# A macaron hybrid layer on one core: outputs of the down projection added in DRAM by DMAs, and a third Strassen set in two more pairs of groups of each FFN

## The chip, the cores and the metric

The kernel runs on one core of a Trainium2 chip. The metric is the time of one execution on the device in microseconds (us). Five engines run in parallel, each its own instructions in order: TensorE (PE: matmuls into PSUM; PEld is its weight load), VectorE (DVE), ScalarE (ACT), GpSimd (POOL) and SyncE (SP, here only issuing DMAs). They wait for each other through semaphores. DMAs issued by GpSimd can add to what stands at their destination in DRAM; those are called accumulating below.

## What is computed

One decoder layer on 256 tokens of width 2048, in float32: a half-step SwiGLU FFN (inner width 5632), a layer norm, a mixer (sliding-window attention beside a convolution, one projection in and one out), a layer norm, a second half-step FFN, a layer norm.

```python
def swiglu_ffn(x, w_gate, w_up, w_down):
    h = jax.nn.silu(x @ w_gate) * (x @ w_up)
    return h @ w_down
...
    x = layer_norm(DEEPNORM_ALPHA * x + 0.5 * swiglu_ffn(x, ffn1_w_gate[l], ffn1_w_up[l], ffn1_w_down[l]),
                   ln1_g[l], ln1_b[l])
...
    x = layer_norm(DEEPNORM_ALPHA * x + mixed, ln2_g[l], ln2_b[l])
    x = layer_norm(DEEPNORM_ALPHA * x + 0.5 * swiglu_ffn(x, ffn2_w_gate[l], ffn2_w_up[l], ffn2_w_down[l]),
                   ln3_g[l], ln3_b[l])
```

## The kernel before

**Precision.** Each float32 operand is split into a high and a low part. ScalarE casts the high part (line 170), VectorE subtracts it for the low part (line 174), and each product of two blocks is three matmuls into the same PSUM bank (`mm3`, lines 677 to 679).

**The FFN's stages.** The inner width is worked in three parts (`PARTS`). Each part has an up stage and then a down stage. The up stage computes gate and up columns in groups of 512 columns (256 of each); groups are numbered 0 to 21, and after the first two (FFN 1) or four (FFN 2) plain groups they come in pairs: 2, 4 and 6 in part one (4 and 6 in FFN 2), 8, 10, 12, 14 in part two, 16, 18, 20 in part three. `pair` makes one. The down stage multiplies the part's inner columns by the down weights. Its output has 4 column blocks of 512 (`NC_`), taken two at a time: column pair `c` = 0, then `c` = 2. In parts one and two both column pairs go through `down_by_sums`; in part three only the first does.

**Sets.** A pair of groups, and a column pair of a down stage, is 8 sets (6 in part three's down stage) of two blocks along the contraction for two token blocks and two column blocks. A "C" set is made plainly with 8 products, 24 matmuls. An "S" set is made after Strassen and Winograd with 7 products, 21 matmuls. An S set's weights need four more subtractions on VectorE (line 188, tiles `sum` and `more`), and three wide and two narrow splits become its four sources: one of 1024 columns as loaded, one of two times 512, one of 1024 and one of 512. A C set needs two splits of 1024. `UP` holds three orders of a pair of groups: the first two have two S sets, the third has three. `up_of` picks one: the first for the pair after the plain groups, the third for the first pair of parts two and three (groups 8 and 16), the second otherwise. `KINDS` gives the down stage's order, "SCCSCSCC" in parts one and two.

**Banks.** `by_sums` holds eight banks of PSUM. Products 1, 5, 6 and 7 occur in S sets alone; after the last S set, `shared` makes four partial sums of them (tiles `part`): ScalarE copies bank 1 scaled by `factor` (line 944), VectorE adds banks 6, 5, 7 and 5 (line 938; line 1077 in the up stage). Banks 2, 4, 3 and 0 go on collecting in the two C sets behind. `out` is called for banks 2 and 4 while the last set runs and for banks 3 and 0 at its end; in the down stage that is `leave`, where VectorE adds the bank to its partial sum (line 938) and GpSimd writes the tile to DRAM: plainly in FFN 1's part one (line 964), accumulating in the other three (line 962). The destination `side` is `y0` or `y1`. The next column pair or pair of groups begins at once in the same banks: its first products are 1, 5, 6, 7, then 2, 4, 3.

**Buffers and order.** The partial sums come from the buffers tagged "z", of which there are `ZB` = 5, as do the activations of the up stage and the sums of the hidden columns. `Steps` plans VectorE's and ScalarE's order: `pace`, called per product, takes the product's time from an estimate of VectorE's backlog, and while that is short lets further weights be split, up to `LEAD` = 7 sources ahead of their use. Weights arrive by SP in four raw buffers (`RAW_BUFS`) or, for S sets, in the tile `more`. In FFN 1, `keep_tokens` reads the layer's input in eight pieces and adds each to `y0` by an accumulating DMA of GpSimd (line 458), at fixed steps; the last falls in part two's first column pair of the down stage. After the last shared sums of an FFN, `tokens_back` loads the sums back from DRAM. GpSimd also writes and reads the transposed hidden columns (lines 1044, 1046).

Of the kernel before, what the change touches and what calls it, by code (L numbers as in the profile page):

```python
# [9 lines left out]
F32 = mybir.dt.float32  # L10
# [4 lines left out]
ALU = mybir.AluOpType  # L15
# [3 lines left out]
P = 128  # L19
# [12 lines left out]
)  # L32
SUMMED = (0, 1, 2)
JG = 2
NC_ = D // 512
# [28 lines left out]
ZB = 5  # L64
# [9 lines left out]


def up_of(g, j0, plain):
    return 0 if g == plain else 2 if g == j0 // JG else 1


def blocks_of(columns):  # L80
    return lambda kind: BLOCKS["L" if kind == "S" and columns < NC_ else kind]
# [265 lines left out]
def hybrid_layer(  # L347
# [3 lines left out]
    nc = tc.nc  # L351
# [4 lines left out]
    act = ctx.enter_context(tc.tile_pool(name="act", bufs=1))  # L356
# [20 lines left out]
    def add_ffn(wu, wd, plain):  # L377
        for (j0, j1), kinds in zip(PARTS, KINDS):
            for g in range(j0 // JG, j1 // JG, 2):
                if g < plain:  # L380
                    sources.extend(wu[g + i, q, h] for i in range(2) for q in range(4) for h in range(2))
                else:
                    for t, kind in UP[up_of(g, j0, plain)]:
                        add_set(kind, [wu[g + i, t // 2, t % 2] for i in range(2)])
            for c in range(0, NC_, 2):
                if c > 0 and j1 == JT:
                    sources.extend(wd[c + i, t // 2, t % 2] for i in range(2) for t in range(j0 // 2, j1 // 2))
                    continue
                for t, kind in enumerate(kinds, j0 // 2):
                    add_set(kind, [wd[c + i, t // 2, t % 2] for i in range(2)])  # L390
# [531 lines left out]
    def down_by_sums(hh, hl, kinds, factor, side, more, columns, last):  # L922

        firsts = [sum(map(blocks_of(columns), kinds[:t])) for t in range(len(kinds))]
        places = {
            "S": ("21", "11", "22", "12", "S1", "S2", "S3", "S4")[-blocks_of(columns)("S"):],
            "C": ("21", "11", "22", "12"),
        }

        def blocks(t, name):  # L930
            n = firsts[t] + places[kinds[t]].index(name)
            return hh[:, n], hl[:, n]

        for c in range(0, columns, 2):
            tmp, places_ = [], {(0, 0): 0, (0, 1): 2, (1, 0): 1, (1, 1): 3}

            def add(out, ps, other):
                nc.vector.scalar_tensor_tensor(out=out, in0=ps, scalar=factor, in1=other, op0=ALU.mult, op1=ALU.add)  # L938
                st.vector(0.62, 0.3)

            def shared(bank, tmp=tmp):

                tmp.extend(act.tile([P, 512], F32, tag="z", name="part", bufs=ZB) for k in range(4))
                nc.scalar.mul(tmp[0], bank[1], factor)
                add(tmp[1], bank[6], tmp[0])
                add(tmp[2], bank[5], tmp[1])
                add(tmp[1], bank[7], tmp[1])
                add(tmp[3], bank[5], tmp[1])
                if last is not None:
                    last()  # L950

            def leave(at, ps, c=c, tmp=tmp):

                t = tmp[places_[at]]
                add(t, ps, t)
                if columns < NC_:
                    y = xts[0][:, 1 - at[0], (c + at[1]) * 512 : (c + at[1] + 1) * 512]
                    joins[1 - at[0], at[1]] = lambda: nc.vector.tensor_tensor(out=y, in0=y, in1=t, op=ALU.add)
                    return
                place = side[1 - at[0], :, (c + at[1]) * 512 : (c + at[1] + 1) * 512]  # L960
                if more:
                    nc.gpsimd.dma_start(place, t, accum_op=ALU.add)
                else:
                    nc.gpsimd.dma_start(place, t)

            by_sums(kinds, blocks, leave, shared)

    def ffn(xc, tag, skew, begun, prepare, finish, places, kept=None):
        with tc.tile_pool(name=f"ffn{tag}", bufs=2) as pool:
            st.act, st.make_places = act, places  # L970
            lhs = (xc[:, :, 0, :], xc[:, :, 1, :])
            xs = pool.tile([P, len(SUMMED), 2, 4, P], F32R, tag="xs", name="xs", bufs=1)

            def sums_of(n):

                k = 2 * SUMMED[n]
                full = act.tile([P, 2, 2, P], F32, tag="z", name="full", bufs=ZB)
                part = act.tile([P, 4, P], F32, tag="z", name="sums", bufs=ZB)
                both = [x_[:, k : k + 2].bitcast(F32) for x_ in lhs]
                nc.vector.tensor_tensor(  # L980
                    out=full.rearrange("p k b n -> p k (b n)"), in0=both[0], in1=both[1], op=ALU.add
                )
                block_sums(part, [full[:, 0, 0], full[:, 0, 1], full[:, 1, 0], full[:, 1, 1]])
                nc.scalar.copy(xs[:, n, 0], part)

                def lower():
                    nc.vector.tensor_tensor(out=xs[:, n, 1], in0=part, in1=xs[:, n, 0].bitcast(F32), op=ALU.subtract)
                    st.vector(0.6)

                if st.paced:  # L990
                    st.soon.append(lower)
                else:
                    lower()
# [10 lines left out]
            def up_blocks(t, name):  # L1004

                if name[0] == "S":
                    return [xs[:, SUMMED.index(t), i, int(name[1]) - 1] for i in range(2)]
                k, b = 2 * t + int(name[1]) - 1, 2 - int(name[0])
                return [x_[:, k, b * P : (b + 1) * P] for x_ in lhs]

            for part, ((j0, j1), kinds) in enumerate(zip(PARTS, KINDS)):
# [109 lines left out]
                while g < j1 // JG:  # L1121
                    if part == 1 and g == j0 // JG:
                        for m in range(2, len(SUMMED)):
                            st.at(4, lambda m=m: st.soon.append(lambda: sums_of(m)))
                    pair(g, UP[up_of(g, j0, plain)])
                    g += 2
                side = sides[xc is not xcat]
                down_by_sums(
                    hh, hl, kinds, 0.5, side, part > 0 or xc is not xcat, columns, (lambda: tokens_back(side)) if ends else None
                )  # L1130
# [466 lines left out]
```

## Time and profile before

| | |
|---|---|
| three runs, median (lowest to highest) | 1674.53 us (1673.40 to 1674.97) |
| the profiled execution | 1675.41 us, span 1673.6 us |
| granted TensorE clock | 0.998 |
| HBM | 349.64 MB read, 27.26 MB written, 225 GB/s |
| GpSimd's DMA queue (q0) | 16112 packets, 45.10 MB, 11.1% of 16 engines |
| ScalarE waits for VectorE's weight subtractions (line 188) | 177.8 us + 158.7 us in all |
| GpSimd waits for VectorE's outputs (line 938, write at line 962) | 172.2 us in all |

The span runs from the first to the last instruction. In the views below, a row of the timeline gives the start, the duration, the engine, the line and operation, the tiles written and read, and in brackets the idle time of the engine before it and who ended it. A row of the groups gives busy time, mean duration in ns, and idle time. A row of the windows gives busy time of each engine and its instructions in a stretch. Starts of matmuls are exact to some ten ns; their ends are modelled.

| stage (us from the span's start) | FFN 1 | FFN 2 |
|---|---|---|
| up, part one, pairs | 49 to 176 | 1052 to 1137 |
| down, part one | 176 to 259 | 1137 to 1220 |
| up, part two (pairs 8, 10, 12, 14) | 259 to 427 | 1220 to 1388 |
| down, part two | 427 to 512 | 1388 to 1471 |
| up, part three (pairs 16, 18, 20) | 512 to 638 | 1471 to 1597 |
| down, part three, first column pair | 638 to 669 | 1597 to 1628 |

### The profile page before, as it was taken

How to read it: one execution, taken by the hardware profiler on the slowest of the kernel's cores; microseconds unless marked ns; L12 is line 12 of the kernel's file. 1: busy time of each engine (PE TensorE's matmuls, PEld its weight loads, DVE VectorE, ACT ScalarE, POOL GpSimd, SP SyncE). 2: the span in 40 equal slices, each digit the busy share in tenths (PEclk: the TensorE clock that was granted, in tenths of full speed). 3: DMA queues.
4: the chain of work that ended last, by engine and by line, in shares of the span. 5: the costliest groups of instructions: out<-in, count | busy, mean ns of one | idle time of the engine just before them, and what ended most of it. 6: DMA issues, size and time to landing. Idle time of an engine off the chain costs nothing. (4 is left out here: it accounts for less than half of the span.)

```text
span 1673.6 us, 21985 instructions
## 1 busy us (share of the span) xinstructions
PE 1657.9 (99%) x7647; PEld 1375.4 (82%) x7647; DVE 1444.1 (86%) x2151; ACT 944.6 (56%) x1316; POOL 323.0 (19%) x302
## 2 busy tenths in 40 slices
PE   9999999999999999999999999999999999999997
PEld 7888888888878888888888888888888888888885
DVE  7899899888999987958888768799999888999877
ACT  6555555555555554676665466455555555556552
POOL 0100000111100001178996201000000000000012
PEclk9999999999999999999999999999999999999999
DMA  8667677677788666656654568666776666776665
GB/s 296 242 227 239 208 250 244 201 249 243 245 242 261 207 225 243 211 189 189 201 176 159 192 226 286 233 223 226 240 244 222 223 222 208 257 235 216 219 238 158
DMA packets 110976, 377.32 MB, mean 225 GB/s; under 512 B 13968, under 2 KB 14096, under 8 KB 110736
## 3 DMA queue, kind: packets, MB, share of 16 engines
q1 hardware_dynamic: 94032, 329.50, 56.6%
q0 software_dynamic: 16112, 45.10, 11.1%
q10 hardware_dynamic: 720, 1.31, 0.2%
q8 instruction: 60, 0.98, 0.2%
q14 instruction: 52, 0.43, 0.1%
HBM read 349.64 MB, written 27.26 MB: 225 GB/s over the span
## 5 line engine op out<-in xcount | busy, mean ns | idle before, releaser
L174 DVE TENSOR_TENSOR lo<-raw,hi 128x1024 fp32r<-128x1024 f32 x320 | 376.1, 1219 | 60.1 <-ACT hi L170 59.9
L677 PE MATMUL sum<-hi,xcat 128*128 128x512 f32 x1006 | 391.6, 389 | 0.4 <-DVE part L1077 0.4
L678 PE MATMUL sum<-lo,xcat 128*128 128x512 f32 x1006 | 391.4, 389 | 0.0
L679 PE MATMUL sum<-hi,xcat 128*128 128x512 f32 x1006 | 391.4, 389 | 0.0
L170 ACT CAST hi<-raw 128x1024 fp32r<-128x1024 f32 x320 | 321.5, 1047 | 59.2 <-DMA raw<-in_wd 19.0
L170 ACT CAST hi<-more 128x1024 fp32r<-128x1024 f32 (+1 forms) x210 | 190.6, 907 | 178.8 <-DVE more L188 158.7
L174 DVE TENSOR_TENSOR lo<-more,hi 128x1024 fp32r<-128x1024 f32 (+1 forms) x210 | 213.7, 1040 | 20.3 <-ACT hi L170 20.2
L677 PE MATMUL sum<-hi,hh 128*128 128x512 f32 x580 | 226.2, 390 | 1.3 <-DVE part L938 1.0
L678 PE MATMUL sum<-lo,hh 128*128 128x512 f32 x580 | 225.7, 389 | 0.0
L679 PE MATMUL sum<-hi,hl 128*128 128x512 f32 x580 | 225.7, 389 | 0.0
L677 PEld LDWEIGHTS sum<-hi,xcat 128*128 128x128 f32 x1006 | 188.8, 188 | 40.4 <-DVE part L1077 1.2
L679 PEld LDWEIGHTS sum<-hi,xcat 128*128 128x128 f32 x1006 | 188.8, 188 | 39.4
L678 PEld LDWEIGHTS sum<-lo,xcat 128*128 128x128 f32 x1006 | 188.8, 188 | 39.0
L253 ACT CAST hi<-raw 128x1024 fp32r<-128x1024 f32 (+1 forms) x156 | 158.5, 1029 | 93.2 <-PE acc L679 42.2
L256 POOL TENSOR_TENSOR lo<-raw,hi 128x1024 fp32r<-128x1024 f32 x73 | 175.9, 2436 | 111.6 <-ACT hi L253 104.8
L170 ACT CAST hi<-sum 128x512 fp32r<-128x512 f32 x140 | 86.8, 622 | 191.4 <-DVE sum L188 177.8
L1044 POOL DMA_DIRECT2D far<-hr x88 | 49.2, 564 | 753.0 <-DVE hr L1039 753.0
L677 PEld LDWEIGHTS sum<-hi,hh 128*128 128x128 f32 x580 | 108.8, 188 | 25.8 <-ACT hi L170 1.3
L679 PEld LDWEIGHTS sum<-hi,hl 128*128 128x128 f32 x580 | 108.9, 188 | 22.7
L678 PEld LDWEIGHTS sum<-lo,hh 128*128 128x128 f32 x580 | 108.9, 188 | 22.6 <-DVE lo L174 0.2
L1077 DVE TENSOR_TENSOR part<-sum,part 128x512 f32<-128x512 f32 x152 | 101.0, 687 | 26.8 <-PE sum L679 19.4
L256 DVE TENSOR_TENSOR lo<-raw,hi 128x1024 fp32r<-128x1024 f32 (+1 forms) x83 | 97.7, 1198 | 25.7 <-ACT hi L253 25.5
(210 smaller groups left out, 2436.1 us busy)
## 6 DMA issues: line engine op xcount, KB each, us to landing
raw<-in_wu SPq DMA_DIRECT2D x264, 512.0 KB, 5.0
raw<-in_wd SPq DMA_DIRECT2D x120, 512.0 KB, 5.3
more<-in_wu SPq DMA_DIRECT2D x84, 512.0 KB, 7.0
more<-in_wd SPq DMA_DIRECT2D x56, 512.0 KB, 7.3
raw<-in_win SPq DMA_DIRECT2D x52, 512.0 KB, 3.9
raw<-in_wout SPq DMA_DIRECT2D x32, 512.0 KB, 4.0
far<-hr POOLq DMA_DIRECT2D x88, 128.0 KB, 2.7
hf<-far POOLq DMA_DIRECT2D x22, 512.0 KB, 3.6
```

The lines of the kernel that those rows point to most:

```text
L170: self.nc.scalar.copy(hi, x_)
L174: self.nc.vector.tensor_tensor(out=lo, in0=x_, in1=hi.bitcast(F32), op=ALU.subtract)
L253: nc.scalar.copy(hi, raw)
L256: eng.tensor_tensor(out=lo, in0=raw, in1=hi.bitcast(F32), op=ALU.subtract)
L677: nc.tensor.matmul(ps, s_hi, m_hi, start=start, stop=False)
L678: nc.tensor.matmul(ps, s_hi, m_lo, start=False, stop=False)
L679: nc.tensor.matmul(ps, s_lo, m_hi, start=False, stop=stop)
L1044: nc.gpsimd.dma_start(far[:, :, t].rearrange("f r n -> r f n"), hr[32 * t : 32 * t + 32])
L1077: nc.vector.tensor_tensor(out=out, in0=ps, in1=other, op=ALU.add)
```

## The change

Two things. A tuple `THREE` names the pairs of groups with three S sets, so groups 12 and 20 of each FFN take the order of groups 8 and 16. And in the down stages of parts one and two, the four partial sums are written to DRAM as soon as `shared` has made them (as plain writes in FFN 1's part one, else accumulating); each output is then copied from its bank by ScalarE, times `factor`, into a "z" tile of its own (`rest`) and added in DRAM by an accumulating DMA. VectorE's last addition (line 938) falls away there. Part three's down stage stays as it was.

```diff
+THREE = (8, 12, 16, 20)
...
 def up_of(g, j0, plain):
-    return 0 if g == plain else 2 if g == j0 // JG else 1
+    return 0 if g == plain else 2 if g in THREE else 1
...
                 if last is not None:
                     last()
+                else:
+                    for at, k in places_.items():
+                        write(at, tmp[k], more)
+
+            def write(at, t, adds, c=c):
+
+                place = side[1 - at[0], :, (c + at[1]) * 512 : (c + at[1] + 1) * 512]
+                if adds:
+                    nc.gpsimd.dma_start(place, t, accum_op=ALU.add)
+                else:
+                    nc.gpsimd.dma_start(place, t)
 
             def leave(at, ps, c=c, tmp=tmp):
 
                 t = tmp[places_[at]]
-                add(t, ps, t)
                 if columns < NC_:
+                    add(t, ps, t)
                     y = xts[0][:, 1 - at[0], (c + at[1]) * 512 : (c + at[1] + 1) * 512]
                     joins[1 - at[0], at[1]] = lambda: nc.vector.tensor_tensor(out=y, in0=y, in1=t, op=ALU.add)
                     return
-                place = side[1 - at[0], :, (c + at[1]) * 512 : (c + at[1] + 1) * 512]
-                if more:
-                    nc.gpsimd.dma_start(place, t, accum_op=ALU.add)
-                else:
-                    nc.gpsimd.dma_start(place, t)
+                t = act.tile([P, 512], F32, tag="z", name="rest", bufs=ZB)
+                nc.scalar.mul(t, ps, factor)
+                write(at, t, True)
```

Since the third S set has two sources more than a C set, the sources behind it are numbered two higher, and lines below the first addition move by one, those below `leave` by ten.

Where FFN 1's second down stage passes from its first column pair to its second, ScalarE's order before was this (`hi` with a number is the high part of that source; in brackets the semaphores awaited, DMASW being those of GpSimd's DMAs and DMAHW those of SP's):

```order
L944 ACTIVATE part_4059<-sum_3782 128x512 [waits DMASW0_49]
L170 CAST hi226_4084<-more_446 128x1024 [waits DVE_49,DMAHW2_49,PE_49,Activation_49]
L170 CAST hi227_4096<-more_446 128x512 [waits DVE_49,PE_49]
L170 CAST hi228_4109<-raw228_3995 128x1024 [waits DMAHW3_49,PE_49,Activation_49]
L170 CAST hi229_4121<-raw229_4007 128x1024 [waits DMAHW4_49,PE_49,Activation_49]
L170 CAST hi230_4156<-raw230_4013 128x1024 [waits DMAHW5_49,PE_49,Activation_49]
L170 CAST hi231_4168<-raw231_4027 128x1024 [waits DMAHW6_49,PE_49,Activation_49]
```

With the change ScalarE's order at the same place is:

```order
L945 ACTIVATE part_4086<-sum_3809 128x512 [waits DMASW0_49]
L171 CAST hi228_4115<-more_446 128x1024 [waits DVE_49,DMAHW2_49,PE_49,Activation_49]
L171 CAST hi229_4127<-more_446 128x512 [waits DVE_49,PE_49]
L171 CAST hi230_4140<-raw230_4022 128x1024 [waits DMAHW3_49,PE_49,Activation_49]
L973 ACTIVATE rest_4144<-sum_3812 128x512 [waits PE_49]
L171 CAST hi231_4150<-raw231_4034 128x1024 [waits DMAHW4_49,Activation_49]
L973 ACTIVATE rest_4164<-sum_3813 128x512 [waits DMASW0_49,PE_49,Activation_49]
L973 ACTIVATE rest_4179<-sum_3814 128x512 [waits DMASW1_49,PE_49]
L973 ACTIVATE rest_4182<-sum_3814 128x512 [waits DMASW2_49]
L171 CAST hi232_4194<-raw232_4040 128x1024 [waits DMAHW5_49]
L171 CAST hi233_4197<-raw233_4054 128x1024 [waits DMAHW6_49]
```

The four copies stand among the weight casts of the next column pair, the second, third and fourth behind waits for DMAs of GpSimd, and two casts that stood directly behind the others now stand behind all four.

GpSimd's order at the same place before (`some` is a piece of the layer's input, `part` a finished output):

```order
L454 DMA some_3967<-in_x 128x512 [waits DMASW6_49]
L458 DMA y0_137<-some_3967 128x512 [waits DMASW7_49,Activation_49]
L962 DMA y0_137<-part_4059 128x512 [waits DVE_49]
L962 DMA y0_137<-part_4060 128x512 [waits DVE_49]
L962 DMA y0_137<-part_4061 128x512 [waits DVE_49]
L962 DMA y0_137<-part_4062 128x512 [waits DVE_49]
```

And with the change (`part` is now a partial sum, `rest` the copy of a bank):

```order
L455 DMA some_3994<-in_x 128x512 [waits DMASW6_49]
L459 DMA y0_137<-some_3994 128x512 [waits DMASW7_49,Activation_49]
L960 DMA y0_137<-part_4086 128x512 [waits Activation_49]
L960 DMA y0_137<-part_4088 128x512 [waits DVE_49]
L960 DMA y0_137<-part_4087 128x512 [waits DVE_49]
L960 DMA y0_137<-part_4089 128x512 [waits DVE_49]
L960 DMA y0_137<-rest_4144 128x512 [waits DMASW4_49,DMASW0_49,Activation_49]
L960 DMA y0_137<-rest_4164 128x512 [waits DMASW5_49,DMASW2_49,Activation_49]
L960 DMA y0_137<-rest_4179 128x512 [waits DMASW6_49,DMASW1_49,Activation_49]
L960 DMA y0_137<-rest_4182 128x512 [waits DMASW7_49,DMASW3_49,Activation_49]
```

The four early writes now follow the last piece of the layer's input directly, and each late write waits for the early write of its own place. VectorE's order up to the shared sums of this column pair is the same rows before and after; behind them its four last additions are gone.

## The prediction

> **What bounds the kernel now.** I read the page's busy line first, then TensorE's timeline where it pauses, then the queues of VectorE, ScalarE and GpSimd at that place.
>
> ```profile
> span 1673.6 us, 21985 instructions
> PE 1657.9 (99%) x7647; PEld 1375.4 (82%) x7647; DVE 1444.1 (86%) x2151; ACT 944.6 (56%) x1316; POOL 323.0 (19%) x302
> ```
>
> TensorE is busy for 99% of the span, so the time falls only if TensorE gets fewer matmuls or loses a pause. The largest pause inside an FFN stands where FFN 1's second down stage passes from its first pair of column blocks to its second (TensorE's timeline; start, duration):
>
> ```profile
> 461.78 0.39 PE L678 MATMUL sum<-lo,hh 128*128 128x512 f32 x1
> ...
> 471.53 0.39 PE L679 MATMUL sum<-hi,hl 128*128 128x512 f32 x1
> 471.86 0.50 PE L677 MATMUL sum<-hi,hh 128*128 128x512 f32 x1
> ...
> 473.68 0.47 PE L677 MATMUL sum<-hi,hh 128*128 128x512 f32 x1 [0.86 <-DVE part L938]
> ...
> 474.79 0.49 PE L677 MATMUL sum<-hi,hh 128*128 128x512 f32 x1 [0.17 <-DVE part L938]
> ```
>
> From the first to the second row there are 43 steps in 9.75 us: 0.2267 us per matmul. In a new pair, products 1, 5, 6 and 7 (12 matmuls) come first, then product 2 (the row at 471.86), product 4 (473.68) and product 3 (474.79). These three need the PSUM banks of the old pair's outputs. Unhindered, product 2 was due at 471.76, so the pair began at 471.76 - 12 x 0.2267 = 469.04; product 4 was due at 472.44, product 3 at 473.12. Product 3 is 1.67 us late. VectorE's timeline shows why:
>
> ```profile
> 464.13 2.94 DVE L938 SCALAR_TENSOR_TENSOR part<-sum,part 128x512 f32<-128x512 f32 x4
> ...
> 471.12 0.68 DVE L938 SCALAR_TENSOR_TENSOR part<-sum,part 128x512 f32<-128x512 f32 x1
> ...
> 472.86 1.87 DVE L938 SCALAR_TENSOR_TENSOR part<-sum,part 128x512 f32<-128x512 f32 x3
> ```
>
> The first row is the four shared additions, the next two are the four outputs; the last ends at 474.73, and product 3 starts at 474.79. Here VectorE frees the banks too late.
>
> **Part one: four Strassen sets more.** Groups 12 and 20 of each FFN get a third "S". An S set has 7 products where a "C" has 8, so 3 matmuls fall away: 4 x 3 x 0.2267 = **2.72 us off TensorE**, all on the path. What the other engines pay (groups by line; busy us, mean ns):
>
> ```profile
> L174 DVE TENSOR_TENSOR lo<-raw,hi 128x1024 fp32r<-128x1024 f32 x320 | 376.1, 1219 | 60.1 <-ACT hi L170 59.9
> L174 DVE TENSOR_TENSOR lo<-more,hi 128x1024 fp32r<-128x1024 f32 (+1 forms) x210 | 213.7, 1040 | 20.3 <-ACT hi L170 20.2
> L174 DVE TENSOR_TENSOR lo<-sum,hi 128x512 fp32r<-128x512 f32 x140 | 90.4, 686 | 0.0
> L188 DVE TENSOR_TENSOR sum<-more,sum 128x512 f32<-128x512 f32 x70 | 48.4, 692 | 2.4
> ...
> L188 DVE TENSOR_TENSOR sum<-more 128x512 f32<-128x512 f32 x70 | 47.2, 675 | 4.8 <-DMA more<-in_wu 2.9 <-DMA more<-in_wd 1.9
> L938 DVE SCALAR_TENSOR_TENSOR part<-sum,part 128x512 f32<-128x512 f32 x80 | 53.4, 685 | 2.6 <-PE sum L679 0.6
> L170 ACT CAST hi<-raw 128x1024 fp32r<-128x1024 f32 x320 | 321.5, 1047 | 59.2 <-DMA raw<-in_wd 19.0 <-DMA raw<-in_wu 17.8 <-ACT hi L170 12.2
> L170 ACT CAST hi<-more 128x1024 fp32r<-128x1024 f32 (+1 forms) x210 | 190.6, 907 | 178.8 <-DVE more L188 158.7 <-PE sum L679 9.1 <-DMA more<-in_wu 4.1
> L170 ACT CAST hi<-sum 128x512 fp32r<-128x512 f32 x140 | 86.8, 622 | 191.4 <-DVE sum L188 177.8 <-PE sum L679 11.0
> L944 ACT ACTIVATE part<-sum 128x512 f32<-128x512 f32 x10 | 5.9, 590 | 0.0
> ```
>
> There are 70 S sets (the two kinds of L188 shown are the ends of four alike). VectorE per S: (213.7 + 90.4 + about 191) / 70 = 7.07 us; per C: 2 x 376.1 / 320 = 2.35 us; each exchange costs it 4.72 us. ScalarE: (190.6 + 86.8) / 70 - 2 x 321.5 / 320 = 1.95 us. The number of weight loads does not change. Is VectorE now late in these pairs of groups? (Windows of one pair each, FFN 1's groups 12, 14, 16 and 20, and the last down pair made by sums.)
>
> ```profile
> core 0: us, PE busy (x) PEld busy (x) DVE busy (x) ACT busy (x) POOL busy (x), PEclk, DMA share, GB/s
> 342.31:384.47 42.16, 42.16 (x188) 34.91 (x186) 36.99 (x50) 24.26 (x32) 5.75 (x9) 1.00 0.79 250
> 384.47:426.63 42.16, 42.16 (x188) 34.91 (x186) 34.92 (x49) 23.49 (x32) 5.74 (x9) 1.00 0.75 227
> 512.33:553.81 41.48, 41.48 (x184) 34.35 (x183) 38.32 (x48) 23.00 (x29) 3.52 (x4) 1.00 0.75 231
> 595.97:638.13 42.16, 42.16 (x187) 34.91 (x186) 37.62 (x50) 23.38 (x30) 2.77 (x5) 1.00 0.67 227
> 638.13:669.41 31.28, 31.28 (x139) 25.90 (x138) 23.43 (x30) 15.92 (x20) 4.93 (x9) 1.00 0.66 233
> ```
>
> Groups 12 would need 36.99 + 4.72 = 41.7 of 41.5 us, groups 20 42.3. That is up to 0.9 us over, but part of an S's preparation falls before its own window, groups 16 already run three S with TensorE full, and the windows behind have 7.2 and 7.9 us of VectorE to spare. I take nothing; without that cover it is 0.2 to 0.9 us in each of four places, about 2 us.
>
> **Part two: 32 last additions leave VectorE.** Four outputs x 2 column pairs x 2 parts x 2 FFNs = 32 additions x 53.4 / 80 = 21.4 us less, against 18.9 us more from part one: VectorE's total hardly moves. ScalarE gets 32 copies x 0.59 = 18.9 us, at 56% no bound. GpSimd gets 32 accumulating DMAs more. Elsewhere TensorE does not wait for these additions:
>
> ```profile
> PE sum L677 <- DVE part L938: 1.0, 2, 0.9
> ```
>
> So relief can return at most the 1.67 us above. What it adds is a wait: each copy needs a fifth buffer of the five tagged "z". Four are held by the partial sums, until their DMAs have landed; ScalarE stands still meanwhile, with the bank not freed and the later weight casts queued behind. In the order above the first copy takes the free buffer, the second to fourth wait for the landings of the first, second and third of the four early writes. ScalarE and GpSimd at this place today:
>
> ```profile
> 467.82 1.05 ACT L170 CAST hi<-more 128x1024 fp32r<-128x1024 f32 x1 [3.73 <-DVE more L188]
> 469.56 0.62 ACT L170 CAST hi<-more 128x512 fp32r<-128x512 f32 x1 [0.68 <-DVE more L188]
> 470.08 3.89 ACT L170 CAST hi<-raw 128x1024 fp32r<-128x1024 f32 x4
> ```
>
> ```profile
> 459.81 0.87 POOL L458 DMA_DIRECT2D y<-some  x1 [14.30 <-ACT some L457]
> 472.24 0.88 POOL L962 DMA_DIRECT2D y<-part  x1 [11.56 <-DVE part L938]
> 473.94 1.75 POOL L962 DMA_DIRECT2D y<-part  x2 [0.82 <-DVE part L938]
> 478.58 0.89 POOL L962 DMA_DIRECT2D y<-part  x1 [2.88 <-DVE lo L174]
> ...
> DMA to landing us min/median/max: 8.4/8.4/8.4
> ...
> DMA to landing us min/median/max: 6.0/8.7/9.8
> ...
> DMA to landing us min/median/max: 5.7/6.8/8.9
> ```
>
> The landings are those of the write at 459.81, of the four here, and of four in FFN 2 (1179 to 1187). The fourth write here was ready at 474.73 but issued at 478.58, just after the first had landed (472.24 + 6.0): the queue holds three accumulating writes. A write is issued 0.43 us after its sum (471.12 + 0.68 to 472.24).
>
> In the changed kernel, on the same clock: first early write 464.5, landing 470.5; second 466.0 (after the second addition), landing with the median 8.7 at 474.7; the third finds three in the queue until the write of 459.81 lands at 468.2, is issued at 468.5, and lands at 477.2. ScalarE: casts to 470.2, one cast of a C weight to 471.1, first copy to 471.7 (in time for product 2); one more cast to 472.7, second copy to 473.3; third from 474.7 to 475.3; fourth from 477.2 to 477.8. Product 3 starts near 477.9, **4.8 us late against 1.67 today: +3.1 us**. Bounds: with no wait for buffers the fourth copy still ends at 474.5 (1.5 late, -0.2); with the 6.8 of FFN 2 it is 475.9, +1.2; with 9.8, +4.2. I take 8.7, the row of this place. VectorE then waits for the casts behind the copies, in time that its outputs took before. On GpSimd the late writes wait for the early ones of their places and may hold its queue some 15 us; behind them stand the next pair's early writes, 30 us on, or the writes of the next pair of groups, 40 us on.
>
> The other seven ends have earlier sums. In FFN 2's first:
>
> ```profile
> 1171.48 2.94 DVE L938 SCALAR_TENSOR_TENSOR part<-sum,part 128x512 f32<-128x512 f32 x4
> ...
> 1137.03:1178.51 41.48, 41.48 (x184) 34.35 (x183) 37.41 (x50) 23.31 (x32) 2.77 (x5) 1.00 0.66 223
> ```
>
> The sums start 7.0 us before the pair's end (4.9 above), so the third write leaves at 1174.2, lands at 1181.0 to 1182.0, and the fourth copy ends up to 1182.7, where product 3 is due at 1178.51 + 4.08 = 1182.6: +0.1. The pair that follows the late one inherits some of it: 0 to 0.9, I take 0.3. The rest: nothing, with 0.4 to 3 us in hand.
>
> **Sum:** -2.72 + 3.1 + 0.1 + 0.3 = +0.8 us. The profiled run took 1675.41 us for its span of 1673.6; on the median of 1674.53 that makes 1675.3.
>
> The Trainium skill, "DMA: Bandwidth & Descriptors", section "Anatomy of one DMA — SWDGE (gpsimd) path", fits a GpSimd DMA as 2.0 us plus bytes / 436e3, an estimate of 2.6 us for these 256 KB; by that the buffers would be free in time and the sum -2.9, as in the first rival. The 6.0 to 9.8 us measured here speak against it.
>
> **The rivals.** (1) *Landings hidden* (20%): early writes land within some 6 us, as the 5.7 of FFN 2 does, and the third is not held up. Only ScalarE's order counts: -2.72 - 0.2 = -2.9, 1671.6. (2) *Relief reaches TensorE* (10%): the sums come 3 us or more earlier, the old pause goes: -2.72 - 1.67 = -4.4, 1670.1. Against it: VectorE's order ahead of those sums is unchanged. (3) *Accumulating DMAs land later everywhere* (12%), since twice as many read and write the same rows of DRAM and share the engines with the weights (busy 0.6 to 0.8 in the windows). From about 0.4 us later the other ends of column pairs stall too; at 1 us later: 1.0 each at the late place, its successor and FFN 2's first, 0.6 at FFN 2's second: +3.6, 1678.9. (4) *VectorE becomes the bound* of the S-rich groups (8%): +2, 1677.3. That the change does nothing is out: the order shows the new sets and copies.
>
> **Chances.** My forecast has 50%. A measurement of this kernel tells about 0.2% (3.3 us) from no change. Faster by that takes rival 2 and half of rival 1's lower part: 0.18. Slower takes most of rival 3, part of 4 and the top of the forecast's own range (9.8 us landings): 0.2. Within: 0.62. The forecast's own range, from the bounds of its large term, is 1672.0 to 1676.4; the range for 8 in 10 has the times of rivals 2 and 3 as ends, 1670.1 to 1678.9.
>
> **What would show it.** TensorE has 12 matmuls fewer; the wait of product 3 at about 477 names ScalarE's copy and has grown to 4 or 5 us; ScalarE idles before its second to fourth copies for a DMA; groups 12 and 20 stay full. Wrong, if that wait is under 2 us, or if TensorE pauses at several other ends or inside groups 12 and 20.

## The result, and the profile after

| | before | changed |
|---|---|---|
| median of 6 runs each (lowest to highest) | 1673.66 us (1673.12 to 1674.97) | 1682.09 us (1679.86 to 1686.86) |
| the profiled execution | 1675.41 us, span 1673.6 | 1679.86 us, span 1678.1 |
| granted TensorE clock | 0.998 | 0.997 |

The ratio is 1.0052, interval [1.0037, 1.0066]: the changed kernel is 8.4 us slower, above the range of the prediction. The profiled execution is the fastest of its six; a second profile of the same kernel has a span of 1681.1 us.

The page of the changed kernel, its span and busy time:

```profile
span 1678.1 us, 22065 instructions
...
PE 1656.7 (99%) x7635; PEld 1374.0 (82%) x7635; DVE 1444.9 (86%) x2147; ACT 964.4 (57%) x1360; POOL 350.4 (21%) x334
```

TensorE has 12 matmuls fewer, VectorE's total has hardly moved, ScalarE has 19.8 us more. What TensorE waits for (engine and line, who is waited for: us in all, times, longest):

```profile
PE sum L678 <- ACT rest L973: 4.4, 3, 3.1
PE sum L680 <- DVE hl L1063: 2.4, 2, 1.2
PE acc L679 <- DVE lo L257: 1.7, 2, 0.9
```

In the first row, 0.70 and 3.10 us are the wait that the prediction is about; the third wait, 0.56 us, stands at FFN 2's second change of pairs. The second row is new, and nothing in the prediction speaks of it. The third stands at FFN 2's end, where the kernel before has a row like it (1.1 us).

**The change of column pairs in FFN 1's second down stage.** TensorE's timeline:

```profile
467.94 0.39 PE L678 MATMUL sum<-hi,hh 128*128 128x512 f32 x1
...
472.19 0.50 PE L678 MATMUL sum<-hi,hh 128*128 128x512 f32 x1 [0.70 <-ACT rest L973]
...
476.28 0.80 PE L678 MATMUL sum<-hi,hh 128*128 128x512 f32 x1 [3.10 <-ACT rest L973]
...
477.30 0.63 PE L680 MATMUL sum<-hi,hl 128*128 128x512 f32 x1
477.72 0.63 PE L678 MATMUL sum<-hi,hh 128*128 128x512 f32 x1
...
479.31 0.39 PE L679 MATMUL sum<-lo,hh 128*128 128x512 f32 x1
```

The new pair began at 467.94, so product 3 was due 18 matmuls later, at 472.02. It came at 476.28, 4.26 us late. Behind it the steps are 0.43 us instead of 0.227 (477.30 to 477.72). The windows say why (the last three columns are the granted clock, the DMA share and GB/s):

```profile
467.94:476.20 8.26, 4.53 (x19) 3.06 (x17) 4.53 (x5) 4.78 (x8) 2.56 (x3) 0.97 1.10 256
476.20:479.00 2.80, 2.72 (x6) 2.15 (x7) 1.81 (x2) 2.80 (x4) 0.86 (x1) 0.50 1.03 368
```

In all 2.8 us of the second window TensorE was granted half its clock. ScalarE's and GpSimd's timelines, and the landings of the first three early writes (us from issue):

```profile
469.89 0.58 ACT L973 ACTIVATE rest<-sum 128x512 f32<-128x512 f32 x1
...
471.55 0.60 ACT L973 ACTIVATE rest<-sum 128x512 f32<-128x512 f32 x1
474.79 0.60 ACT L973 ACTIVATE rest<-sum 128x512 f32<-128x512 f32 x1 [2.65 <-DMA y<-part]
475.63 0.60 ACT L973 ACTIVATE rest<-sum 128x512 f32<-128x512 f32 x1 [0.24 <-DMA y<-part]
```

```profile
458.66 0.89 POOL L459 DMA_DIRECT2D y<-some  x1 [14.30 <-ACT some L458]
463.37 0.89 POOL L960 DMA_DIRECT2D y<-part  x1 [3.82 <-ACT part L945]
464.79 0.86 POOL L960 DMA_DIRECT2D y<-part  x1 [0.53 <-DVE part L939]
467.88 0.86 POOL L960 DMA_DIRECT2D y<-part  x1 [2.23 <-DVE lo L175]
```

```profile
y<-part POOLq DMA_DIRECT2D x1, 256.0 KB, 8.1
...
y<-part POOLq DMA_DIRECT2D x1, 256.0 KB, 9.9
...
y<-part POOLq DMA_DIRECT2D x1, 256.0 KB, 7.7
```

Each copy starts just behind a landing: 463.37 + 8.1 = 471.47 and the second copy at 471.55; 464.79 + 9.9 = 474.69 and the third at 474.79; 467.88 + 7.7 = 475.58 and the fourth at 475.63. The named releaser of the third early write (VectorE) had long been done; the write stood behind three others, and was issued 0.3 us after the first of them, that of 458.66, had landed at 467.56.

**The new wait.** TensorE and VectorE in FFN 1's last part, at the first low parts of the hidden columns of groups 20 (tile `hl`):

```profile
660.95 0.39 PE L679 MATMUL sum<-lo,hh 128*128 128x512 f32 x1
662.53 0.50 PE L680 MATMUL sum<-hi,hl 128*128 128x512 f32 x1 [1.19 <-DVE hl L1063]
```

```profile
612.12 4.63 DVE L175 TENSOR_TENSOR lo<-raw,hi 128x1024 fp32r<-128x1024 f32 x4 [0.26 <-ACT hi L171]
...
640.60 0.69 DVE L1087 TENSOR_TENSOR part<-sum,part 128x512 f32<-128x512 f32 x1
...
645.64 2.36 DVE L175 TENSOR_TENSOR lo<-raw,hi 128x1024 fp32r<-128x1024 f32 x2 [0.29 <-ACT hi L171]
647.92 1.42 DVE L1035 TENSOR_TENSOR ht<-part 128x256 f32<-128x256 f32 x4
...
657.25 4.63 DVE L175 TENSOR_TENSOR lo<-raw,hi 128x1024 fp32r<-128x1024 f32 x4
661.79 1.29 DVE L1063 TENSOR_TENSOR hl<-hf,hh 128x512 fp32r<-128x512 f32 x2
```

VectorE works from 612.12 to 645.3 without a wait, across the end of groups 20, and is never idle from there to `hl`. In the kernel before, it waited for work at the same end:

```profile
634.02 1.23 DVE L174 TENSOR_TENSOR lo<-raw,hi 128x1024 fp32r<-128x1024 f32 x1 [0.79 <-ACT hi L170]
...
638.33 1.29 DVE L1077 TENSOR_TENSOR part<-sum,part 128x512 f32<-128x512 f32 x2 [1.89 <-PE sum L679]
...
657.20 1.28 DVE L1053 TENSOR_TENSOR hl<-hf,hh 128x512 fp32r<-128x512 f32 x2
```

Measured from the start of the down stage (638.13 before, 640.29 after), `hl` starts at 19.07 us before and at 21.50 us after. TensorE needs the first half at 661.18 - 640.29 = 20.9 us and the half takes 0.7 us: some 1.1 us of margin before, 1.3 us late after. The pause comes again in FFN 2 (1619.6).

**Where the time went.** The table adds up, for each place, the steps between starts of matmuls less 0.227 us. "Again" is the second profile of the changed kernel; the other columns are the experiments below.

| us lost at | before | changed | again | sets only | writes only | own buffers | without 20 | own, without 20 | own, 18 |
|---|---|---|---|---|---|---|---|---|---|
| FFN 1's second down, change of pairs | 1.77 | 5.70 | 6.16 | 1.77 | 6.08 | 1.07 | 6.59 | 1.03 | 1.04 |
| the last `hl`, both FFNs | 0 | 2.91 | 2.92 | 2.92 | 0 | 2.91 | 0 | 0 | 0 |
| FFN 2's second down, change of pairs | 0 | 0.83 | 1.03 | 0 | 0 | 0 | 0.31 | 0 | 0 |
| FFN 2's end, near 1650 | 1.60 | 2.38 | 3.08 | 2.23 | 1.70 | 2.93 | 1.49 | 2.23 | 1.17 |
| start of FFN 1's second down | 0.79 | 1.06 | 1.32 | 1.13 | 0 | 0.75 | 1.05 | 0.97 | 0.48 |
| groups 4, both FFNs | 1.72 | 0 | 0.59 | 1.53 | 1.29 | 4.38 | 0.94 | 3.82 | 2.07 |
| start of the kernel | 0.39 | 0.28 | 1.23 | 0.55 | 0.84 | 0.86 | 1.09 | 0.80 | 0.33 |
| fewer matmuls | 0 | -2.72 | -2.72 | -2.72 | 0 | -2.72 | -1.36 | -1.36 | -2.72 |
| span | 1673.6 | 1678.1 | 1681.1 | 1675.9 | 1677.0 | 1677.7 | 1677.4 | 1675.0 | 1669.8 |

From before to the second profile the rows differ by 4.39 + 2.92 + 1.03 + 1.48 + 0.53 - 1.13 + 0.84 - 2.72 = +7.3 us; the spans differ by 7.5. The rows of groups 4 and of the kernel's start move from profile to profile in kernels whose programs don't differ there. The two largest at groups 4, 4.38 and 3.82, come from profiled runs of 1679.52 and 1676.74 us, the second slowest and the slowest of their kernels. The start costs more where TensorE's clock becomes whole later: 3.9 us into the span in the kernel before, 6.8 us in the second profile.

### The profile page after: what moved, and what is told of

It is laid out like the page before. It is cut to its first block, busy times and chain, and to the rows that moved or that the text cites. A ratio compares the mean times of both kernels' runs of the same rounds, so it can differ in the third digit from the quotient of the medians.

```text
span 1678.1 us, 22065 instructions
## 1 busy us (share of the span) xinstructions
PE 1656.7 (99%) x7635; PEld 1374.0 (82%) x7635; DVE 1444.9 (86%) x2147; ACT 964.4 (57%) x1360; POOL 350.4 (21%) x334
## 5 line engine op out<-in xcount | busy, mean ns | idle before, releaser
L175 DVE TENSOR_TENSOR lo<-raw,hi 128x1024 fp32r<-128x1024 f32 x312 | 367.0, 1220 | 55.2 <-ACT hi L171 55.1
L678 PE MATMUL sum<-hi,xcat 128*128 128x512 f32 x986 | 383.6, 389 | 0.0
L680 PE MATMUL sum<-hi,xcat 128*128 128x512 f32 x986 | 383.6, 389 | 0.0
L679 PE MATMUL sum<-lo,xcat 128*128 128x512 f32 x986 | 383.6, 389 | 0.0
L171 ACT CAST hi<-raw 128x1024 fp32r<-128x1024 f32 x312 | 313.0, 1047 | 42.5 <-DMA raw<-in_wd 16.8
L171 ACT CAST hi<-more 128x1024 fp32r<-128x1024 f32 (+1 forms) x222 | 201.5, 908 | 226.1 <-DVE more L189 189.6
L175 DVE TENSOR_TENSOR lo<-more,hi 128x1024 fp32r<-128x1024 f32 (+1 forms) x222 | 226.9, 1042 | 41.3 <-ACT hi L171 40.8
L679 PEld LDWEIGHTS sum<-lo,xcat 128*128 128x128 f32 x986 | 185.1, 188 | 38.6
L680 PEld LDWEIGHTS sum<-hi,xcat 128*128 128x128 f32 x986 | 185.1, 188 | 38.5
L678 PEld LDWEIGHTS sum<-hi,xcat 128*128 128x128 f32 x986 | 185.1, 188 | 38.2
L171 ACT CAST hi<-sum 128x512 fp32r<-128x512 f32 x148 | 90.8, 622 | 152.8 <-DVE sum L189 138.7
```

What stands on the lines that cost most here:

```text
L171: self.nc.scalar.copy(hi, x_)
L175: self.nc.vector.tensor_tensor(out=lo, in0=x_, in1=hi.bitcast(F32), op=ALU.subtract)
L678: nc.tensor.matmul(ps, s_hi, m_hi, start=start, stop=False)
L679: nc.tensor.matmul(ps, s_hi, m_lo, start=False, stop=False)
L680: nc.tensor.matmul(ps, s_lo, m_hi, start=False, stop=stop)
```

## The experiments

Each was timed in five rounds beside the kernel before. Those in the first four paragraphs shared one set of runs of before (median 1674.59 us), the next four another (1675.51), the last two a third (1674.51).

**The sets alone (sets_only).** The kernel before, with the third Strassen set in groups 12 and 20 and nothing else.

```diff
+THREE = (8, 12, 16, 20)
-    return 0 if g == plain else 2 if g == j0 // JG else 1
+    return 0 if g == plain else 2 if g in THREE else 1
```

> The four third S sets alone, the outputs as before. Theory A (the loss comes from ScalarE's copies waiting for buffers at the change of column pairs in FFN 1's second down stage, and from the slower clock behind that pause): nothing of it is left, TensorE has 12 matmuls less, so 1.0 to 2.7 us under the kernel before. Theory B (part of the loss comes from the third S in groups 20, which makes VectorE late, so that the low parts of the last hidden columns come late in part three's down stage): a pause of about 1.3 to 1.6 us in each FFN at the first use of those columns, naming VectorE's subtraction for them; 0 to 1 us over the kernel before. The old pause of 1.7 us at the change of column pairs stays in both.

Measured: 1677.51 us, ratio 1.0019 [1.0010, 1.0028]. Twelve matmuls fewer, and the kernel is 2.9 us slower, more than the 0 to 1 us expected. Both `hl` pauses are there at their full 1.45 us, the old pause at 471 is unchanged. So the sets make the new pauses by themselves. FFN 2's end and the start of FFN 1's second down stage lose another 0.6 and 0.3 us in this profile; the pauses alone don't make up the 2.9.

**The writes alone (writes_only).** The changed kernel with the third set where it was before.

```diff
-THREE = (8, 12, 16, 20)
+THREE = (8, 16)
```

> Early writes, copies and accumulating DMAs, but groups 12 and 20 with two S sets. Theory A: the pause at the change of column pairs in FFN 1's second down stage stays near 4.3 us for product 3 against 1.7 before, with the clock halved for some 2.8 us behind it, and a pause near 0.9 us stands in FFN 2's; 4 to 8 us over the kernel before. Theory B: no pause of 1.5 us in part three's down stages; if B were the main cause the time is within 2 us of the kernel before. Rival C (twice as many accumulating DMAs slow all transfers): pauses for weights, over 4 us more, spread over several stages.

Measured: 1678.97 us, 1.0030 [1.0018, 1.0041]. The pause at the change of pairs is 6.08 us, with half the clock behind it, and there is no `hl` pause. The 0.9 us expected at FFN 2's second change of pairs did not come. The two parts alone add up to 0.49%, the whole is 0.52%: within the intervals their costs add up.

**Buffers of their own for the copies (own_buffers).** The changed kernel, but the second to fourth copy of a column pair go to three buffers that no DMA of a partial sum holds.

```diff
-                t = act.tile([P, 512], F32, tag="z", name="rest", bufs=ZB)
+                if at == (0, 0):
+                    t = act.tile([P, 512], F32, tag="z", name="rest", bufs=ZB)
+                else:
+                    t = st.own.tile([P, 512], F32, tag="rest", name="rest", bufs=3)
```

> The changed kernel, with three buffers of their own for the second to fourth copy, so that no copy waits for an early write. Theory A: product 3 is then late only by ScalarE's order, about 1.5 us, no slower clock behind; 4 to 6 us under the changed kernel, 1676 to 1678. Theory B: the two pauses of 1.5 us in part three's down stages stay. Rival C: the same DMAs run, so the time stays within 2 us of the changed kernel, near 1682.

Measured: 1676.85 us, 1.0012 [1.0003, 1.0020]. The pause falls to 1.07 us, less than the 1.77 us of before, and the clock stays whole there. The writes, copies and DMAs are all still there; only the wait for a buffer is gone. So that wait, with the half clock behind it, is the cost of the second part.

**No third set in groups 20 (without_20).** The changed kernel with `THREE = (8, 12, 16)`.

```diff
-THREE = (8, 12, 16, 20)
+THREE = (8, 12, 16)
```

> The changed kernel with the third S in groups 12 only. Theory B: the two pauses in part three's down stages go (3.0 us), six matmuls come back (+1.4), so about 1.7 us under the changed kernel. Theory A: the pause in FFN 1's second down stage stays as it was, 4.3 us. If neither pause changes, B is wrong and the time is 1.4 us over the changed kernel.

Measured: 1679.23 us, 1.0026 [1.0016, 1.0036]. Both `hl` pauses are gone and the change of pairs loses 6.59 us. Groups 20, not groups 12, make the new pauses.

**The changed kernel again (after_again),** to have a second profile of it.

> The changed kernel itself, on the same chip as the three others. Both theories: 5 to 9 us over the kernel before; product 3 waits 4 to 5 us for ScalarE's copy in FFN 1's second down stage with the clock halved behind it, and each part three's down stage has a pause of 1.5 us for the low parts of the last hidden columns.

Measured: 1682.89 us, 1.0048 [1.0034, 1.0061]; the profile is the column "again" above. The pauses at the change of pairs, at `hl` and in FFN 2's second down stage came again.

**Both undone (own_without_20).** The kernel with buffers of its own for the copies, and no third set in groups 20.

```diff
-THREE = (8, 12, 16, 20)
+THREE = (8, 12, 16)
```

> Buffers of their own for the copies, and the third S in groups 12 only: both suspected causes are gone. If these two are all, nothing is left of the loss and TensorE has 6 matmuls less (1.4 us) and up to 1 us less of the old pause: 0 to 2.4 us under the kernel before, about 1673. Rival C (the DMAs themselves, or VectorE late in general): still 1 us or more over the kernel before.

Measured: 1673.19 us, 0.9990 [0.9981, 0.9999]. The loss of the change is gone, with all of its early writes and copies still in place.

**An earlier last set in groups 20 (own_order_20).** With own buffers, groups 20 take an order whose third S stands one set earlier, to test whether the place of the last S makes `hl` late.

```diff
+    ((0, "S"), (3, "C"), (1, "S"), (4, "C"), (2, "S"), (5, "C"), (6, "C"), (7, "C")),
...
-    return 0 if g == plain else 2 if g in THREE else 1
+    return 0 if g == plain else 3 if g == 20 else 2 if g in THREE else 1
```

> As own_buffers, but groups 20 have their three S sets as the first, third and fifth set, so that the last S is a set earlier and three C sets follow it. If the late hidden columns come from the place of the last S (its shared sums and the outputs behind them, queued behind weight splits), the pauses of 1.5 us in part three's down stages shrink below 0.5 us and the time falls by 2 to 3 us against own_buffers, to about the kernel before. If they come from VectorE's load alone, which is the same, they stay at 1.3 to 1.6 us.

Measured: 1681.68 us, 1.0042 [1.0030, 1.0055]. The `hl` pauses stay at 1.45 us, and in each FFN new pauses of 1.7 us come at 620 and 641, where TensorE waits for low parts and for `part` of VectorE. That the place of the last S were the cause is refuted: in this order VectorE was late sooner, and at `hl` still.

**Earlier pieces of the layer's input (early_pieces).** The changed kernel, with the pieces of `keep_tokens` spaced by 7 steps in place of 8, so that none stands in GpSimd's queue ahead of the early writes.

```diff
-            st.at(96 + 8 * n, one, True)
+            st.at(96 + 7 * n, one, True)
```

> The changed kernel, with the pieces of the layer's input added at 7 instead of 8 steps, so that the last is through some 15 us before the early writes. If the full queue of accumulating writes holds the third early write back (issued at 467.9 in the changed kernel, ready at 465.2), it is now issued at once, lands 2 to 3 us earlier, and the wait of product 3 falls from 4.3 to 2 to 3 us, without a slower clock: 2 to 3.5 us under the changed kernel. If the landings are long because the DMA engines are busy with weights, the third copy still waits for the second write near 474.7, and the time stays within 1 us.

Measured: 1685.05 us, 1.0060 [1.0047, 1.0073]. At the change of pairs, the third early write goes out right behind the second (GpSimd's timeline), and the loss falls to 1.67 us:

```profile
473.01 1.75 POOL L960 DMA_DIRECT2D y<-part  x2 [0.56 <-DVE part L939]
```

That does not show that the queue's hold on the third write made the lateness. The first three early writes also land sooner here, in 7.0, 6.8 and 7.3 us. In the changed kernel the third copy waited for the second write, which no queue held, to 474.79; with the third write sooner and nothing else, the fourth copy would have started some 0.3 us earlier, right behind the third (an estimate: it waited 0.24 us behind the third). So the shorter landings are the larger part; what shortened them was not tried by itself.

The last piece now comes beside the writes of the hidden columns, and ScalarE stands still for it (ScalarE's and TensorE's timelines, then windows of TensorE alone: busy time, granted clock, DMA share, GB/s):

```profile
441.19 1.05 ACT L171 CAST hi<-more 128x1024 fp32r<-128x1024 f32 x1
449.31 0.63 ACT L458 ACTIVATE some<-some 128x512 f32<-128x512 f32 x1 [7.07 <-DMA some<-in_x]
```

```profile
450.50 0.50 PE L678 MATMUL sum<-hi,hh 128*128 128x512 f32 x1 [2.46 <-ACT hi L171]
```

```profile
448.42:451.83 3.41, 1.11 (x4) 1.00 0.03 12
451.83:455.24 3.41, 3.41 (x10) 0.50 1.00 131
```

TensorE pauses from the matmul at 447.65 to 450.50, and again loses half its clock afterwards: 4.8 us in all by 455.2. Smaller pauses near 387, 419 and 464 lose another 2.3 us. This is a miss as a remedy, and the clearest case of the clock.

**A third set in groups 18 instead of 20 (own_18).** Both undone as above, and one set more in the pair before the last.

```diff
-THREE = (8, 12, 16)
+THREE = (8, 12, 16, 18)
```

> The kernel is own_without_20 (copies of the last products in buffers of their own, third S in groups 8, 12 and 16) with one third S more, in groups 18, the pair before the last of part three's up stage. Theory A: what makes the pauses of about 1.5 us before the first use of the last pair's hidden columns is three S in the part's last pair, groups 20, alone; then no such pause comes in either FFN's second part, TensorE has 6 matmuls fewer in each FFN's part three (12 x 0.2267 / 2 = 1.4 us), and the time is about 1.4 us under own_without_20's, 0.9982 of the kernel before. Theory B: VectorE's load in the whole end of part three decides, and a third S in groups 18 hands the same 4 us on to the last pair; then pauses of 1.2 to 1.6 us come at both places (about 660 and 1619 us) and the time is about 1.6 us over own_without_20's, 1.0000 of the kernel before.

Measured: 1672.11 us, 0.9983 [0.9975, 0.9992]. No `hl` pause comes. VectorE's timeline and the windows of groups 18, 20 and the down stage behind (span, then busy time of PE, PEld, DVE, ACT, POOL, clock, DMA share, GB/s):

```profile
631.57 1.22 DVE L175 TENSOR_TENSOR lo<-raw,hi 128x1024 fp32r<-128x1024 f32 x1 [0.18 <-ACT hi L171]
...
635.88 1.29 DVE L1090 TENSOR_TENSOR part<-sum,part 128x512 f32<-128x512 f32 x2 [1.89 <-PE sum L680]
...
654.74 1.28 DVE L1066 TENSOR_TENSOR hl<-hf,hh 128x512 fp32r<-128x512 f32 x2
```

```profile
552.04:593.51 41.47, 41.47 (x184) 34.36 (x183) 40.80 (x56) 24.02 (x32) 2.84 (x5) 1.00 0.65 225
593.51:635.67 42.16, 42.16 (x187) 34.92 (x186) 39.57 (x53) 24.46 (x32) 2.75 (x5) 1.00 0.75 245
635.67:666.96 31.29, 31.29 (x140) 25.91 (x139) 24.25 (x31) 15.65 (x20) 4.93 (x9) 1.00 0.67 238
```

With three S, VectorE is busy for 40.80 of 41.47 us in groups 18, more than the 38.37 of 41.48 us that it had in groups 20 of the changed kernel, and nothing is lost: groups 20 behind take up the rest, VectorE waits for work again before their end, and `hl` starts 654.74 - 635.67 = 19.07 us into the down stage, as before. ScalarE's copies at the old pause no longer wait:

```profile
469.97 0.59 ACT L976 ACTIVATE rest<-sum 128x512 f32<-128x512 f32 x1
470.46 1.04 ACT L171 CAST hi<-raw 128x1024 fp32r<-128x1024 f32 x1
471.40 1.57 ACT L976 ACTIVATE rest<-sum 128x512 f32<-128x512 f32 x3
```

This version has the same 7635 matmuls as the changed kernel, and beats both: 2.8 us under the kernel before, with an interval of 1.3 to 4.2 us. What it should gain, 2.72 us of matmuls and 1.77 - 1.04 = 0.73 us at the old pause, lies inside.

**Groups 12 by themselves (sets_12).** The kernel before with `THREE = (8, 12, 16)`.

```diff
+THREE = (8, 12, 16)
-    return 0 if g == plain else 2 if g == j0 // JG else 1
+    return 0 if g == plain else 2 if g in THREE else 1
```

> The kernel before with a third S in groups 12 alone (8, 12, 16), the outputs' last additions on VectorE as before. Theory A: groups 12 has a whole window of VectorE's spare time behind it and no hidden columns are due at its end; then nothing is lost, 6 matmuls fewer in each FFN are worth 1.4 us, 0.9992 of the kernel before, and no pause over 1 us stands in the second down stages but the old one at 471 us (1.77 us). Theory B: a third S costs VectorE's 4 us somewhere wherever it stands; then a new pause stands in part two and the ratio is 1.0000 or above.

Measured: 1674.05 us, 0.9995 [0.9986, 1.0004]. The profile has no new pause and the old one at 1.75 us. The 1.36 us of six matmuls lie inside the interval, but so does no gain at all: by the trace groups 12 cost nothing, by the time it is unclear.

## Why the prediction was wrong

**"All on the path", -2.72 us.** Right: 7635 matmuls for 7647. The version with a third set in groups 18 has the same number and is 2.8 us faster than before, though 0.73 us of that is the old pause's.

**"I take nothing" for the third sets.** This is the step that failed. The argument was that the windows behind groups 12 and 20 have 7.2 and 7.9 us of VectorE to spare. For groups 12 the trace bears it out. For groups 20 it does not: that spare lies in the whole window behind, but the low parts of the part's last hidden columns are due 20.9 us into it, behind work of VectorE that leaves no gap. Only some 1.1 us could be late there. The windows hid this too: groups 20 look slack after the change (38.37 of 41.48 us), because their work ran over into the next window.

```profile
598.81:640.29 41.48, 41.48 (x185) 34.35 (x183) 38.37 (x53) 22.62 (x30) 2.75 (x5) 1.00 0.59 204
640.29:673.09 32.80, 31.61 (x140) 25.75 (x138) 26.43 (x34) 17.31 (x23) 4.93 (x9) 1.00 0.70 241
```

The busy time of the second window rose from 23.43 to 26.43 us. It cost 1.45 us in each FFN, 2.9 in all. The fourth rival named VectorE, but priced its excess inside four groups; the place was another. "Groups 12 and 20 stay full" was fulfilled and told nothing.

**"+3.1 us" at the change of column pairs.** The mechanism was right, step by step: a third early write held by the queue, the second to fourth copy each behind a landing, product 3 late by 4.26 us where 4.8 was said. The landings of 8.1, 9.9 and 7.7 us stand against 6.0, 8.7 and 8.7 assumed. The hold of the third write decided less than was said: it landed 0.9 us after the second, not 2.5. The size of the term was off: 5.70 - 1.77 = +3.9 us in one profile and +4.4 in the other. The lateness alone grew by 4.26 - 1.67 = 2.6 us; the rest is what follows a long pause, mostly the half clock, which the prediction did not have.

**"The rest: nothing, with 0.4 to 3 us in hand".** Wrong in one of these places: FFN 2's second change of pairs lost 0.83 and 1.03 us, none with own buffers and none without the new third sets. There the shared sums of VectorE start 6.2 and 6.8 us before the next pair begins, against 7.2 in the kernel with the writes alone; so here the third set in groups 12, ahead of this stage, may add to what the copies wait (without groups 20 the loss was 0.31 us). The 0.1 and 0.3 us put on FFN 2's first change and on the pair behind the late one did not come.

**Not in the sum: FFN 2's end.** There TensorE waits for VectorE's low parts of weights (line 257 in the changed kernel). The six profiles with a third S in groups 20 lose 2.2 to 3.2 us, the six others 1.2 to 2.2, before among them. The ranges meet, so whether that set is the cause, and how it would reach so far, is open.

**The rivals.** *Landings hidden* fell with the 7.7 to 9.9 us measured. That is three to four times the 2.6 us estimated from the fit of the Trainium skill, "DMA: Bandwidth & Descriptors", section "Anatomy of one DMA — SWDGE (gpsimd) path". *Relief* came only where the copies had their own buffers, and then as 0.7 of the 1.77 us. *Landings later everywhere* would have shown at FFN 2's first change too, which loses nothing: the first three early writes landed there in 6.4 to 6.9 us, the first three writes of before in 5.7 to 7.7.

With the sizes of the second profile the sum is -2.72 + 4.4 + 2.9 + 1.0 + 1.5 (FFN 2's end) + 0.5 (start of FFN 1's second down) = +7.6 us, near the 8.4 of the medians; -1.1 of groups 4 and +0.8 of the kernel's start, which move without the change, are left out.

## What to carry to other kernels

Slack of an engine in a window is worth something only up to the next moment at which its work is due; look in the queue for that moment, not at the window's share. A buffer that is given to a DMA early is held until the DMA lands, so a copy that takes the same pool waits for the landing; three small buffers of their own undid it. In this kernel a third set cost 1.45 us in the last pair of a stage and nothing one pair earlier, where a pair of the same kind behind it takes up the backlog; when work is added to a stage, try it one step ahead of the end.

## What the runs showed of the hardware

**The clock after a pause.** Pauses of up to 2.37 us between the starts of two matmuls left TensorE's clock alone; such a one stands in the kernel with own buffers:

```profile
1097.18 0.39 PE L680 MATMUL sum<-hi,xs 128*128 128x512 f32 x1
1099.56 0.50 PE L678 MATMUL sum<-hi,xcat 128*128 128x512 f32 x1 [1.99 <-DVE part L1090]
1099.89 0.39 PE L679 MATMUL sum<-lo,xcat 128*128 128x512 f32 x1
```

All five of 2.85 to 4.38 us inside the FFNs were followed by five to seven matmuls at 0.427 us, from up to 1.3 us after the pause (447.65 to 450.50 above, half clock from 451.83). Each of the five half clocks lasted 3.41 us, and the stretch of whole clock ahead of it 131 or 138 times as long. In the 3.41 us just ahead of a half clock TensorE was busy for 1.11 us at most (the window at 448.42 above); beside the pause of 2.37 us it was busy for 2.10 us of such a window, and the clock stayed whole (TensorE alone):

```profile
1098.38:1101.79 3.41, 2.10 (x8) 1.00 0.82 234
```

The Trainium skill, "TensorE: Matmul & The Clock Gate", section "Part 1: The HAM clock gate (the "warmup" mystery)", says that the clock is halved after at least one idle window of about 3.4 us, and that the windows run free. That the half clocks last 3.41 us, with whole multiples of it ahead of them, and begin at changing distances from the pauses agrees with such windows. That a pause of 2.85 us was enough, with 1.11 us of work in its window, does not agree with a whole idle window.

**GpSimd's queue.** With one write of the layer's input in it, two early writes went out and the third waited (2.23 us); without that piece three went out at once. Both fit a queue that holds three such accumulating writes. In the whole profile of the changed kernel none was issued with three other accumulating ones under way, and 27 were issued 0.31 us after a landing that left two. The limit is not one of DMAs as such: the four plain writes of FFN 1's part one went out at once, at 209.57, 211.03, 211.82 and 212.55, the first landing at 215.79.
